# A hybrid decoder trunk on one core: attention scores of a head pair as one full-array product on a block diagonal key tile

## The chip, the cores and the metric

The kernel runs on one core of one Trainium2 chip. Such a core has a matrix engine (TensorE, PE in the profile, with its weight loads as PEld), a vector engine (VectorE, DVE), an activation engine (ScalarE, ACT), a general engine (GpSimd, POOL), and DMA queues that the sync engine (SyncE, SP) issues. The engines run side by side; each executes its own instructions in order and waits on semaphores of the others. The metric is the device time of one execution in microseconds (us), as a median over runs.

## What is computed

Two layers of a conditioned decoder trunk on 256 positions with width 1024. Each layer has a mixer, in which a gated delta rule branch (8 heads) and a sliding-window attention branch (16 query heads, 2 key heads, head width 64, window 128) stand side by side, and then a gated MLP of width 2816. All inputs and weights are fp32. The part of the reference that the change touches, cut:

```python
def swa_sink_attention(q, k, v, sinks):
    qb = q.astype(f32).reshape(B, nb, SWA_BLOCK, SWA_KV_HEADS, SWA_GROUP, D)
    kb, vb = band(k), band(v)
    s = jnp.einsum('bnqhgd,bnkhd->bnhgqk', qb, kb) * (D ** -0.5)
    ...
    s = jnp.where(mask[None, :, None, None], s, -jnp.inf)
    m = jnp.maximum(jnp.max(s, axis=-1, keepdims=True), sink)
    p = jnp.exp(s - m)
    denom = jnp.sum(p, axis=-1, keepdims=True) + jnp.exp(sink - m)
    o = jnp.einsum('bnhgqk,bnkhd->bnqhgd', p / denom, vb)
```

## The kernel before, in words

Most of the time goes to projections. A chunk of 128 x 1024 weights comes in by DMA as `raw`, ScalarE casts it to a reduced-precision high part `wH` (line 210), VectorE subtracts to get the low part `wL` (line 212), and `mm3` (lines 282 to 284) adds three products of 128 x 256 for each of the eight slices: high times high, high times low, low times high. The modulation vectors come from dot products of a 128 x 1024 chunk `wada` on VectorE (line 328), which shares the `raw` buffers.

Everything else of the mixer is put between these products. A small planner in the kernel (`Job`, `spawn`, `tick`, lines 230 to 258) advances generators by estimated cost and wait, a number pair at each `yield`; the framework's scheduler then sets each engine's final order, ahead of time, from the dependencies, buffers and priorities. Among the generators are the delta rule's two halves of four heads (`Half`: Gram products `ps_kk` at line 728, a blocked triangular inverse with the tiles `u`, `ut`, `yt` and products `ps_y`, `ps_z`, then the solve), and the attention.

The attention has two parts. `attention_prep(tb)` (line 932) normalizes and rotates queries and keys for one block of 128 positions and transposes them: `qT` holds for each of eight head pairs 128 rows, 64 of the even and 64 of the odd head; `kT` holds each key head's transposed keys twice, in rows 0 to 63 and again in rows 64 to 127. ScalarE copies the transposed keys from PSUM to `kT` (line 967).

`attention(tb, kv)` (line 969) is one unit: a block of 128 queries and a key head, that is eight query heads. There are four units per layer. The scores go to two tiles of four heads, `ps_cur0` for the even and `ps_cur1` for the odd heads, each 128 x 512. Line 975 issues eight products, one per head, alternating between the two tiles: 64 rows of `qT` as the stationary side, 64 rows of `kT` as the moving side with 128 columns. In the profile these have the tile `64*128`. A unit of the first block (tb = 0) has only this set; one of the second block has a second set against the previous block's keys (`ps_prv`, line 987), written over the masked places by `copy_predicated`. The tiles come from the PSUM pool `atps`, which has two buffers, shared with the value products `ps_o`, the transposed probabilities `ps_pT`, and tiles of the delta rule (`ps_vt`, `ps_n2`).

Then come maximum, exponential with the row sum, division (lines 994 to 1012), a transposition of the probabilities on PE (line 1016) into `pc` and, in the second block, `pp`, and the product with the values: line 1031, for even heads into partitions 0 to 63 of `ps_o` and for odd heads into 64 to 127, each of 512 columns (four heads at once), and line 1034 for the previous block, added on. In the profile these have the tile `128*64`.

Buffers that the change renames: `ssq` (line 411), a running sum of squares for the norms, has a tag of its own; `k2` (line 697), squares of keys in the delta rule, has one buffer; `pc` at line 442, a column of a rank-one correction, has four buffers of four bytes a partition.

Of the kernel before, what the change touches and what calls it, by code (L numbers as in the profile page):

```python
# [4 lines left out]
F32 = mybir.dt.float32  # L5
# [7 lines left out]
P = 128  # L13
T = 256
# [85 lines left out]
def trunk(tc, xT, cvec, pos, wada, wsa, wbig, wdn, par, cst, out):  # L100
# [15 lines left out]
    big = pool("big", 1)  # L116
    wk = pool("wk", 2)
# [291 lines left out]
    def ssq_add(kt):  # L409
        if kt == 0:  # L410
            s = wk.tile([P, T], F32, name="ssq", tag="ssq", bufs=1)
            A.activation(s, x[:, 0], AF.Square)
            ssq["t"] = s
        else:
            q = t1("sqx")
            A.activation(q, x[:, kt], AF.Square)
            V.tensor_tensor(ssq["t"], ssq["t"], q, ALU.add)

    class Raw:
# [16 lines left out]
        def proj(self, r, scale=1.0, alt=False):  # L436

            p_ = proj(lambda kt: self.h[:, kt, 0:T + 2], lambda kt: self.l[:, kt, 0:T + 2], T + 2, alt)
            with tc.high_priority(offset=HPN):
                t = t1("pr")  # L440
                V.tensor_tensor(t, p_[:, 0:T], r, ALU.mult)
                c = sm.tile([P, 1], F32, name="pc", bufs=4)
                A.activation(c, p_[:, T:T + 1], AF.Identity, scale=scale)
            return t, c
# [79 lines left out]
    for l in range(NL):  # L524
# [407 lines left out]
        def attention_prep(tb):  # L932
# [32 lines left out]
            for g in range(2):  # L965
                PE.transpose(pk[:, g], kd[:, g].rearrange("p a b -> p (a b)"), C("ident"))
            A.copy(kT[:, :, ts], pk)

        def attention(tb, kv):
            ts = slice(tb * P, tb * P + P)  # L970
            hfs = (slice(0, 64), slice(64, 128))
            pcur = [pat([4, P], name=f"ps_cur{i}") for i in range(2)]
            for j in range(4):
                for i in range(2):
                    PE.matmul(pcur[i][:, j], qT[hfs[i], kv * 4 + j, ts], kT[hfs[i], kv, ts], start=True, stop=True)  # L975
            s_ = [at2(f"s{i}") for i in range(2)]
# [3 lines left out]
            else:  # L980
                for i in range(2):
                    AB.copy(s_[i], pcur[i])
                yield 0.95, 1.2
                pprv = [pat([4, P], name=f"ps_prv{i}") for i in range(2)]
                for j in range(4):
                    for i in range(2):
                        PE.matmul(pprv[i][:, j], qT[hfs[i], kv * 4 + j, ts], kT[hfs[i], kv, 0:P],
                                  start=True, stop=True)
                for i in range(2):
# [4 lines left out]
            for i in range(2):  # L994
                s = s_[i]
                hs = slice(kv * 8 + i, kv * 8 + 8, 2)
                mx = sm.tile([P, 4], F32, name="mx", bufs=4)
# [8 lines left out]
                for j in range(4):  # L1006
                    after(AB.activation(s[:, j], s[:, j], AF.Exp, bias=nm[:, j:j + 1],
                                       scale=rq[:, tb, kv * 8 + i + 2 * j:kv * 8 + i + 2 * j + 1],
                                       accum_out=sme[:, j:j + 1]), last_silu[-1])
# [18 lines left out]
            po = pat([4, P], name="ps_o")  # L1028
            o = [po[i * 64:i * 64 + 64] for i in range(2)]
            for i in range(2):  # L1030
                PE.matmul(o[i], vtok[:, tb, vs], pcs[i], start=True, stop=tb == 0)  # L1031
            if tb:
                for i in range(2):
                    tc.keep_in_program_order(PE.matmul(o[i], vtok[:, 0, vs], pps[i], start=False, stop=True))
            ks = slice(kv * 4, kv * 4 + 4)
# [18 lines left out]
        qT = big.tile([P, 8, T], F32, name="qT", tag="s5")  # L1054
        kT = big.tile([P, 2, T], F32, name="kT", tag="kT")
        rq = sm.tile([P, 2, 16], F32, name="rq")
# [259 lines left out]
```

## Time and profile before

| | us |
|---|---|
| median of 3 runs | 1029.28 |
| lowest and highest run | 1028.52, 1032.02 |
| span of the profiled execution | 1029.4 |
| PE busy, of that span | 999.7 (97%) |
| VectorE busy | 843.6 (82%) |
| ScalarE busy | 631.2 (61%) |
| GpSimd busy | 4.0 |

No separate device time is given for the profiled execution beside its span. In a row of the timeline stand the start, the time, the engine, the line, the operation, output and inputs, the shape, a count, and in brackets the idle time ahead with what ended it. In a row of the groups the count is followed by the busy time in us, the mean of one in ns, and the idle time ahead. In a row of the windows stand the stretch, its length, then for each engine (PE, PEld, DVE, ACT, POOL, unless one is chosen) the busy time with the number of instructions, then the granted clock of PE, the share of the DMA engines, and GB/s. Helpers that raise an operation's priority stand under line 278.

### The profile page before, as it was taken

The page shows a single profiled execution, that of the slowest core. Times are in us where ns is not written, and L with a number is a line of the kernel's source. Part 1 is how long each engine was busy: PE and PEld are TensorE (multiplying, and loading weights), DVE is VectorE, ACT ScalarE, POOL GpSimd, SP SyncE. Part 2 cuts the span into 40 slices and gives each one's busy share as a digit, 9 for nine tenths or more (in the row PEclk, how much of TensorE's full clock was granted, in tenths as well). Part 3 has the DMA queues.
Part 4 walks back from the last instruction along what each step waited for, and adds up shares of the span by engine and source line. Part 5 has one row for each costly group of instructions (what it writes and reads, how often), then busy time and mean ns, then how long its engine had stood idle before and what let it go on. Part 6 is the DMA issues. An engine that isn't in the chain of part 4 may idle for free.

```text
span 1029.4 us, 23195 instructions
## 1 busy us (share of the span) xinstructions
PE 999.7 (97%) x9208; PEld 946.0 (92%) x9208; DVE 843.6 (82%) x1873; ACT 631.2 (61%) x1281; POOL 4.0 (0%) x8
## 2 busy tenths in 40 slices
PE   4999999999999999999999999999999999999998
PEld 2599998998899999999999999899879999999998
DVE  6799997799788898998996999986857889777653
ACT  5598675766555665564465977577554558555532
POOL 0000000000000000000000000000000000000000
PEclk9999998999999999999999999999999999999999
DMA  9875486537555478888976556762313655566661
GB/s 361 324 247 175 173 268 204 183 124 266 170 183 191 155 226 282 291 282 298 358 262 210 168 168 193 239 242 83 110 57 107 202 185 179 191 191 194 185 211 40
DMA packets 60444, 210.47 MB, mean 204 GB/s; under 512 B 6960, under 2 KB 8496, under 8 KB 60336
## 3 DMA queue, kind: packets, MB, share of 16 engines
q1 hardware_dynamic: 59904, 208.89, 61.3%
q8 instruction: 72, 1.18, 0.5%
q14 instruction: 36, 0.29, 0.1%
q10 hardware_dynamic: 432, 0.10, 0.0%
HBM read 207.92 MB, written 1.05 MB: 203 GB/s over the span
## 4 chain that ended last, share of the span: by engine, by line
PE 77%; DVE 13%; ACT 5%; DMA 2%; issue 2%; SPq 0%; DVEq 0%; ACTq 0%
PE acc L282 20%; PE acc L283 19%; PE acc L284 19%; DVE wL L212 4%; PE pa L567 4%; DMA raw<-wada 2%; ACT wH L210 2%; DVE raw L328 2%; PE ps_o L1031 1%; PE ps_kk L728 1%; DVE kq L672 1%; PE ps_cur L975 1%; PE pa L585 1%; PE pa L583 1%; PE pa L584 1%
## 5 line engine op out<-in xcount | busy, mean ns | idle before, releaser
L210 ACT CAST wH<-raw 128x1024 fp32r<-128x1024 f32 (+2 forms) x292 | 301.0, 1035 | 207.8 <-PE acc L283 130.0
L212 DVE TENSOR_TENSOR wL<-raw,wH 128x1024 fp32r<-128x1024 f32 (+2 forms) x292 | 349.3, 1200 | 76.2 <-ACT wH L210 73.3
L282 PE MATMUL acc<-hH,wH 128*128 128x256 f32 x1376 | 394.3, 287 | 0.0
L283 PE MATMUL acc<-hL,wH 128*128 128x256 f32 x1376 | 385.8, 280 | 0.0
L284 PE MATMUL acc<-hH,wL 128*128 128x256 f32 x1376 | 385.1, 280 | 0.3 <-DVE wL L212 0.2
L282 PEld LDWEIGHTS acc<-hH,wH 128*128 128x128 f32 x1376 | 259.9, 189 | 7.4 <-issue 4.3
L284 PEld LDWEIGHTS acc<-hH,wL 128*128 128x128 f32 x1376 | 260.1, 189 | 1.1 <-DVE wL L212 0.7
L283 PEld LDWEIGHTS acc<-hL,wH 128*128 128x128 f32 x1376 | 260.1, 189 | 0.7 <-issue 0.2
L328 DVE SCALAR_TENSOR_TENSOR raw<-raw,cact 128x1024 f32<-128x1024 f32 x80 | 97.1, 1219 | 9.2 <-DMA raw<-wada 9.1
L284 PE MATMUL acc<-g_b,wL 128*128 128x256 f32 x224 | 61.8, 276 | 0.0
L282 PE MATMUL acc<-g_b,wH 128*128 128x256 f32 x224 | 61.8, 276 | 0.0
L283 PE MATMUL acc<-g_b,wH 128*128 128x256 f32 x224 | 61.8, 276 | 0.0
L672 DVE SCALAR_TENSOR_TENSOR kq<-cr,pt,kq 128x255 f32<-128x255 f32 (+2 forms) x96 | 45.4, 479 | 1.5 <-ACT kq L670 1.5
L282 PEld LDWEIGHTS acc<-g_b,wH 128*128 128x128 f32 x224 | 42.1, 188 | 0.0
L283 PEld LDWEIGHTS acc<-g_b,wH 128*128 128x128 f32 x224 | 42.1, 188 | 0.0
L284 PEld LDWEIGHTS acc<-g_b,wL 128*128 128x128 f32 x224 | 42.1, 188 | 0.0
L567 PE MATMUL pa<-raw,h 128*128 128x432 f32 x96 | 37.5, 555 | 2.6 <-ACT h L473 2.6
L1192 DVE SCALAR_TENSOR_TENSOR g<-acc,pt,g 128x255 f32<-128x255 f32 x80 | 38.2, 478 | 0.6
L567 PEld LDWEIGHTS pa<-raw,h 128*128 128x128 f32 x96 | 19.2, 202 | 20.6 <-issue 17.2
L282 PE MATMUL acc<-sH,wH 128*128 128x256 f32 x128 | 36.7, 289 | 0.0
L284 PE MATMUL acc<-sH,wL 128*128 128x256 f32 x128 | 36.6, 287 | 0.0
L283 PE MATMUL acc<-sL,wH 128*128 128x256 f32 x128 | 36.5, 285 | 0.0
(329 smaller groups left out, 1964.0 us busy)
## 6 DMA issues: line engine op xcount, KB each, us to landing
raw<-wbig SPq DMA_DIRECT2D x232, 512.0 KB, 4.0
raw<-wada SPq DMA_DIRECT2D x80, 512.0 KB, 4.5
raw<-wdn SPq DMA_DIRECT2D x32, 512.0 KB, 4.5
raw<-wsa SPq DMA_DIRECT2D x24, 432.0 KB, 4.8
early<-wada SPq DMA_DIRECT2D x16, 512.0 KB, 8.5
raw<-wdn SPq DMA_DIRECT2D x16, 384.0 KB, 4.1
x<-xT SPq DMA_DIRECT2D x4, 256.0 KB, 4.2
out<-x SPq DMA_DIRECT2D x8, 128.0 KB, 3.0
```

The lines of the kernel that those rows point to most:

```text
L210: A.copy(h, raw)
L212: V.tensor_tensor(lo, raw, h.bitcast(F32), ALU.subtract)
L282: PE.matmul(o, wh, ah, start=first, stop=False)
L283: PE.matmul(o, wh, al, start=False, stop=False)
L284: PE.matmul(o, wl, ah, start=False, stop=last)
L328: return V.scalar_tensor_tensor(raw, raw, 1.0, cact, op0=ALU.mult, op1=ALU.mult, accum_out=modp[l][:, f:f + 1])
L567: PE.matmul(pa[g][tb], h32[:, tb * P:tb * P + P], w, start=n == 0, stop=n == KT - 1)
L583: PE.matmul(o, hh[:, kt, sl], wh[:, k4], start=kt == 0, stop=False)
L584: PE.matmul(o, hh[:, kt, sl], wl[:, k4], start=False, stop=False)
L585: PE.matmul(o, hl[:, kt, sl], wh[:, k4], start=False, stop=kt == KT - 1)
L672: V.scalar_tensor_tensor(dst[:, sft:], cr[:, :T - sft], w_[:, 3 - sft:4 - sft], dst[:, sft:], op0=ALU.mult, op1=ALU.add)
L1192: V.scalar_tensor_tensor(g[:, sft:], pa_[:, :T - sft], fw[:, i, 2 - sft:3 - sft], g[:, sft:], op0=ALU.mult, op1=ALU.add)
```

## The change

`kT` is replaced by `kbd`, a tile with, for each key head and each block of 128 keys, 256 columns: rows 0 to 63 hold the transposed keys in the first 128 columns, rows 64 to 127 hold them in the last 128, and the rest is zero, set once per layer by a memset on GpSimd. The copy from PSUM becomes two copies of 64 rows each. A product now takes all 128 rows of a head pair of `qT` as the stationary side and 256 columns of `kbd` as the moving side, and gives the scores of both heads of the pair next to each other: four products in place of eight for a set. So the heads lie in natural order in the score tiles, heads 0 to 3 of the unit in the first and 4 to 7 in the second, each tile filled by two products in a row. The slices of the sinks and of the scales follow. The value products take the even or odd heads of a tile by a stride of two, each with 256 columns, so twice as many. Besides, `ssq` shares the buffer of `k2`, and `pc` has three buffers.

```diff
     def ssq_add(kt):
         if kt == 0:
-            s = wk.tile([P, T], F32, name="ssq", tag="ssq", bufs=1)
+            s = wk.tile([P, T], F32, name="ssq", tag="k2", bufs=1)
...
-                c = sm.tile([P, 1], F32, name="pc", bufs=4)
+                c = sm.tile([P, 1], F32, name="pc", bufs=3)
...
-            A.copy(kT[:, :, ts], pk)
+            for i in range(2):
+                q = slice(i * 64, i * 64 + 64)
+                A.copy(kbd[q, :, tb, i], pk[q])
 
         def attention(tb, kv):
             ts = slice(tb * P, tb * P + P)
-            hfs = (slice(0, 64), slice(64, 128))
-            pcur = [pat([4, P], name=f"ps_cur{i}") for i in range(2)]
-            for j in range(4):
-                for i in range(2):
-                    PE.matmul(pcur[i][:, j], qT[hfs[i], kv * 4 + j, ts], kT[hfs[i], kv, ts], start=True, stop=True)
+
+            def scores(name, blk):
+                out = []
+                for b in range(2):
+                    o = pat([4, P], name=name)
+                    for p_ in range(2):
+                        PE.matmul(o[:, 2 * p_:2 * p_ + 2], qT[:, kv * 4 + 2 * b + p_, ts], kbd[:, kv, blk],
+                                  start=True, stop=True)
+                    out.append(o)
+                return out
+
+            pcur = scores("ps_cur", tb)
...
-                pprv = [pat([4, P], name=f"ps_prv{i}") for i in range(2)]
-                for j in range(4):
-                    for i in range(2):
-                        PE.matmul(pprv[i][:, j], qT[hfs[i], kv * 4 + j, ts], kT[hfs[i], kv, 0:P],
-                                  start=True, stop=True)
+                pprv = scores("ps_prv", 0)
...
-                hs = slice(kv * 8 + i, kv * 8 + 8, 2)
+                h0 = kv * 8 + 4 * i
+                hs = slice(h0, h0 + 4)
...
-                                       scale=rq[:, tb, kv * 8 + i + 2 * j:kv * 8 + i + 2 * j + 1],
+                                       scale=rq[:, tb, h0 + j:h0 + j + 1],
...
             po = pat([4, P], name="ps_o")
-            o = [po[i * 64:i * 64 + 64] for i in range(2)]
-            for i in range(2):
-                PE.matmul(o[i], vtok[:, tb, vs], pcs[i], start=True, stop=tb == 0)
-            if tb:
+            for b in range(2):
+                o = [po[i * 64:i * 64 + 64, 2 * b:2 * b + 2] for i in range(2)]
                 for i in range(2):
-                    tc.keep_in_program_order(PE.matmul(o[i], vtok[:, 0, vs], pps[i], start=False, stop=True))
+                    PE.matmul(o[i], vtok[:, tb, vs], pcs[b][:, i::2], start=True, stop=tb == 0)
+                if tb:
+                    for i in range(2):
+                        tc.keep_in_program_order(PE.matmul(o[i], vtok[:, 0, vs], pps[b][:, i::2], start=False, stop=True))
...
-        kT = big.tile([P, 2, T], F32, name="kT", tag="kT")
+        kbd = big.tile([P, 2, 2, 2, P], F32, name="kbd", tag="kbd")
+        G.memset(kbd, 0.0)
```

The new score products are line 979 of the changed kernel, the value products lines 1038 and 1041, the key copies line 969.

## The prediction

> **What bounds the kernel now.** I read the page first: the busy shares, the granted clock and the chain that ended last.
>
> ```profile
> PE 999.7 (97%) x9208; PEld 946.0 (92%) x9208; DVE 843.6 (82%) x1873; ACT 631.2 (61%) x1281; POOL 4.0 (0%) x8
> PEclk9999998999999999999999999999999999999999
> PE 77%; DVE 13%; ACT 5%; DMA 2%; issue 2%; SPq 0%; DVEq 0%; ACTq 0%
> ```
>
> The span is 1029.4 us, and TensorE (PE) is busy in 97% of it and carries 77% of the chain. So what counts is the time that PE's stream takes, and the few places where the stream stands still. Next come the groups of instructions on PE that the change touches; the last two numbers before the idle time are busy us and mean ns. An fp32 product leaves two records (128 records for the 64 products of L975).
>
> ```profile
> L975 PE MATMUL ps_cur<-kT,qT 64*128 64x128 f32 x128 | 16.0, 291 | 1.6 <-issue 1.6
> L1031 PE MATMUL ps_o<-pc,vtok 128*64 128x512 f32 x32 | 12.4, 618 | 0.0
> L987 PE MATMUL ps_prv<-kT,qT 64*128 64x128 f32 x64 | 7.1, 285 | 0.2 <-ACT s L278 0.2
> L1034 PE MATMUL ps_o<-pp,vtok 128*64 128x512 f32 x16 | 6.5, 598 | 0.0
> ```
>
> About 23 us of scores and 19 us of value products: 4% of the span. A mean of 291 ns is no price, since matmuls overlap; prices I take from starts in the timeline. Here are a half set (four products, one head parity), a whole set (eight, the parities alternating), and full-array fp32 products of 256 columns in another stage (two products).
>
> ```profile
> 220.21 0.28 PE L283 MATMUL acc<-hL,wH 128*128 128x256 f32 x1
> 220.33 0.28 PE L284 MATMUL acc<-hH,wL 128*128 128x256 f32 x1
> 220.54 1.16 PE L975 MATMUL ps_cur<-kT,qT 64*128 64x128 f32 x8
> 221.62 0.39 PE L282 MATMUL acc<-hH,wH 128*128 128x256 f32 x1
> 221.85 0.28 PE L283 MATMUL acc<-hL,wH 128*128 128x256 f32 x1
> ```
>
> ```profile
> 224.83 0.28 PE L284 MATMUL acc<-hH,wL 128*128 128x256 f32 x1
> 225.04 1.16 PE L987 MATMUL ps_prv<-kT,qT 64*128 64x128 f32 x16
> 226.13 0.39 PE L282 MATMUL acc<-hH,wH 128*128 128x256 f32 x1
> 226.36 0.28 PE L283 MATMUL acc<-hL,wH 128*128 128x256 f32 x1
> ```
>
> ```profile
> 106.87 0.28 PE L284 MATMUL acc<-hH,wL 128*128 128x256 f32 x1
> 106.98 1.03 PE L728 MATMUL ps_kk<-kq 128*128 128x256 f32 x4
> 107.66 0.47 PE L282 MATMUL acc<-hH,wH 128*128 128x256 f32 x1
> 107.97 0.28 PE L283 MATMUL acc<-hL,wH 128*128 128x256 f32 x1
> ```
>
> A projection product steps by 0.12 us (220.21 to 220.33). I price a block from the last product before it to the second behind it, less two such steps, which takes in what entering and leaving cost. The half set costs 221.85 - 220.33 - 0.24 = 1.28 us. The whole set, with twice the products, costs 226.36 - 224.83 - 0.24 = 1.29: products on the two 64-row halves run side by side only if they alternate. Two full-array products cost 107.97 - 106.87 - 0.24 = 0.86, that is 0.43 each.
>
> **Scores, product by product.** A unit of the first query block has one set, the current block's; a unit of the second has two, with the previous block's. Two units of each per layer make 6 sets, 12 in all. Whether a set is whole or split is decided by the order. On PE in layer 0, second unit, stood (ps_cur_2500 and ps_cur_2501 are the two score tiles):
>
> ```order
> L975 MATMUL ps_cur_2500<-kT,qT 128x128 x4
> L282 MATMUL acc<-hH,wH 128x256
> L283 MATMUL acc<-hL,wH 128x256
> L284 MATMUL acc<-hH,wL 128x256
> L282 MATMUL acc<-hH,wH 128x256
> L283 MATMUL acc<-hL,wH 128x256
> L284 MATMUL acc<-hH,wL 128x256
> L877 MATMUL ps_y_2520<-vt,um 128x128 x2
> L975 MATMUL ps_cur_2501<-kT,qT 128x128 x4
> ```
>
> and now, at the same place:
>
> ```order
> L979 MATMUL ps_cur<-kbd,qT 128x256 x2
> L282 MATMUL acc<-hH,wH 128x256
> L283 MATMUL acc<-hL,wH 128x256
> L284 MATMUL acc<-hH,wL 128x256
> L282 MATMUL acc<-hH,wH 128x256
> L283 MATMUL acc<-hL,wH 128x256
> L284 MATMUL acc<-hH,wL 128x256
> L877 MATMUL ps_y_2517<-vt,um 128x128 x2
> L979 MATMUL ps_cur<-kbd,qT 128x256 x2
> ```
>
> Four products of one parity wait together for the second buffer and so run alone; two full-array products take the place of each four. In the whole order 5 sets alternate and 7 are split. Three half sets late in layer 1 follow each other and share their entry:
>
> ```profile
> 753.92 0.82 PE L975 MATMUL ps_cur<-kT,qT 64*128 64x128 f32 x5
> ...
> 756.89 0.69 PE L828 MATMUL ps_z<-u,yt 32*32 32x32 f32 x32
> ```
>
> They take 2.97 us and not 3 x 1.28 = 3.84. Before: 5 x 1.29 + 14 x 1.28 - 0.87 = 23.5 us. After: 48 x 0.43 = 20.6. **-2.9 us.** A whole set gets dearer (1.72 for 1.29) and a split one cheaper (1.72 for 2.56).
>
> The Trainium skill, "TensorEngine Tiling (Array Packing)", When to Use Tiling, says that a contraction of 64 should use two row tiles, which may give up to twice the speed. By it the old form would be the better one, by 12 x (1.72 - 1.29) = 5.2 us; the trace agrees for the 5 alternating sets and not for the 7 split ones.
>
> **Value products.** They go from 24 of 512 columns to 48 of 256, as many columns. A pair on the two column halves and a single product cost alike:
>
> ```profile
> 192.07 0.28 PE L284 MATMUL acc<-hH,wL 128*128 128x256 f32 x1
> 192.28 1.08 PE L1031 MATMUL ps_o<-pc,vtok 128*64 128x512 f32 x4
> 193.29 0.38 PE L282 MATMUL acc<-hH,wH 128*128 128x256 f32 x1
> ```
>
> ```profile
> 242.57 1.07 PE L1031 MATMUL ps_o<-pc,vtok 128*64 128x512 f32 x2
> 243.57 0.75 PE L787 MATMUL ps_y<-ut,lq 32*32 32x32 f32 x64
> ```
>
> 1.01 us for the pair, 1.00 for one alone: each broken pair costs another 1.0. On PE in layer 0, third unit (ps_y: the inverse's products), stood
>
> ```order
> L1031 MATMUL ps_o<-pc,vtok 64x512
> L787 MATMUL ps_y_3251<-ut_3243,lq 32x32 x32
> L1031 MATMUL ps_o<-pc,vtok 64x512
> L1034 MATMUL ps_o<-pp,vtok 64x512 x2
> L282 MATMUL acc<-hH,wH 128x256
> ```
>
> and now
>
> ```order
> L1038 MATMUL ps_o<-pc,vtok 64x256 x2
> L1041 MATMUL ps_o<-pp,vtok 64x256
> L787 MATMUL ps_y_3242<-ut_3234,lq 32x32 x32
> L1041 MATMUL ps_o<-pp,vtok 64x256
> L1038 MATMUL ps_o<-pc,vtok 64x256 x2
> L1041 MATMUL ps_o<-pp,vtok 64x256 x2
> ```
>
> The broken pair is now of half the columns. Layer 1 has two such places, so 3 x 0.5 = 1.5 us go. Against this stand 24 more products, whose start no row shows at 256 columns on half the array; bounds are 0 and 24 x 0.07 = 1.7 (an estimate: the pair's 1.01 is two passes after one another, 0.50 each, where 512 columns take 0.43 on the full array). Most of that 0.07 is the entry into the half array, paid once a block, so I take 0.3, near nothing. **-1.2 us.**
>
> **What lies beside PE.** The key copy is cut in two:
>
> ```profile
> L967 ACT COPY kT<-ps_kT x4: 372/372/373, 100.7 to 615.0; 128x256 f32<-128x256 f32 x4
> ```
>
> Four more copies of at most 0.37 are 1.5 us of ScalarE (ACT), busy 61%; behind them wait the weight casts (wH). Bounds 0 and +1.5; I take **+0.3**. The two memsets of kbd go to GpSimd (POOL), whose eight instructions took 4.0 us in all; one stands first in its queue and the other between memsets of the inverse, both long ahead of a reader: nothing, at most their own 1 us each if a score waited. The shared buffers (ssq with k2, three pc) meet in stages that don't overlap: nothing.
>
> **The order in layer 0.** At the first score set stand two stalls:
>
> ```profile
> 164.38 0.71 PE L975 MATMUL ps_cur<-kT,qT 64*128 64x128 f32 x6
> 166.71 1.13 PE L975 MATMUL ps_cur<-kT,qT 64*128 64x128 f32 x10 [1.62 <-issue]
> ...
> 168.37 0.41 PE L284 MATMUL acc<-hH,wL 128*128 128x256 f32 x1
> 169.19 0.34 PE L820 MATMUL ps_y<-ut,lq 32*32 32x32 f32 x5 [0.41 <-DVE ut L278]
> ```
>
> ```profile
> 167.46 1.23 DVE L328 SCALAR_TENSOR_TENSOR raw<-raw,cact 128x1024 f32<-128x1024 f32 x1 [2.81 <-DMA raw<-wada]
> ```
>
> The second: ps_y waits for ut, and ut stands on VectorE (DVE) behind a modulation dot that waits 2.81 us for its DMA. The difference on DVE there (u and ut: the inverse; - before, + now):
>
> ```order
>  L352 SCALAR_TENSOR_TENSOR a_0_109<-mod_102,pt 128x4
> -L278 SCALAR_TENSOR_TENSOR u_1527<-ps_z_2089,ct,u_1527 128x8x16
> -L328 SCALAR_TENSOR_TENSOR raw,modp_104<-raw,cact 128x1024
> -L278 STREAM_TRANSPOSE ut_2148<-u_1527 128x256
> +L278 SCALAR_TENSOR_TENSOR u_1530<-ps_z_2092,ct,u_1530 128x8x16
> +L212 TENSOR_TENSOR wL<-raw,wH 128x1024
>  L672 SCALAR_TENSOR_TENSOR vv<-cr,pt,vv 128x255
> ```
>
> The dot (L328) no longer stands between u and ut; it comes later, when the data has long landed. The wait of 169.19 - 168.37 - 0.12 = 0.7 us goes: **-0.7** (bounds 0, if the wL now ahead is late, and -0.7). The first stall is "issue", inside a run of products that waits for no engine. Six passes stand ahead of it; in the whole set above 16 took 225.04 to 226.13, 0.07 each, and in the new form one takes 0.215. If the stall ends at a fixed moment, 166.71, the new passes fill 6 x (0.215 - 0.07) = 0.9 us of it, less 0.1 for the entry that they don't pay: **-0.8** (bounds 0, if it moves along, and -1.6, if it goes).
>
> **The sum.** -2.9 - 1.2 + 0.3 - 0.7 - 0.8 = -5.3. Some comes back as waits where PE now arrives earlier at ACT or DVE; I take 0.7, from this row of the stage of layer 1 with its scores, where 1.75 us of PE idle time exist already:
>
> ```profile
> 675.00:775.00 100.00, 98.25 (x1111) 1.00 0.32 108
> ```
>
> -4.6 us. The profiled span of 1029.4 is 0.1 above the median of the runs, 1029.28, so I set it against the median: **1024.7 us**. About 0.3% (3.1 us) is what a measurement of this kernel can tell from no change; the runs themselves lay between 1028.52 and 1032.02.
>
> **Rivals.** *Only the stream gets shorter, and part is handed back*: the two order terms don't come, ACT's copies cost their 1.5 and waits return 0.9: -2.9 - 1.2 + 1.5 + 0.9 = -1.7, 1027.6 us. For it: the order of DVE and ACT in layer 0 is shuffled widely from 100 us on, and DVE is in the chain there. Against: the products themselves are priced by rows. Chance 0.30.
>
> *The clock stays up*: behind the stalls at 164 to 169 us the clock falls:
>
> ```profile
> 163.70:167.10 3.40, 1.78 (x18) 1.45 (x20) 0.88 (x5) 3.05 (x7) 0.00 (x0) 1.00 0.87 312
> 167.10:173.90 6.80, 6.39 (x86) 5.61 (x84) 5.54 (x14) 1.27 (x4) 0.00 (x0) 0.50 0.38 133
> ```
>
> After a stretch with PE busy 1.78 of 3.40, 6.8 us run at clock 0.50. With the stalls shortened that stretch would be busy for some 2.6, and at full clock the 6.39 would take 3.2 less; I count 3.0. 1024.7 - 3.0 = 1021.7 us. Against: how much idle time brings the clock down isn't seen. Chance 0.17. The Trainium skill, "TensorE: Matmul & The Clock Gate", Part 1, says that free-running windows of about 3.4 us decide, one idle window bringing half clock; the length agrees with the row, and by it the phase, not the kernel alone, settles this rival.
>
> *Half A comes late* (the other side): the last of its Gram products (ps_kk) moved 23 products back on PE, 23 x 0.12 = 2.7 us, and its inverse starts from that. If its products stand where they stood, PE waits the 2.7, and a second stretch at half clock costs another 3.2: -1.7 + 2.7 + 3.2 = +4.2, 1033.5 us. It decides from about 2 us of wait on. Against: the first ps_y moved back by 12 products too. Chance 0.05.
>
> *The row tiles were the better form*: if the split halves ran side by side after all, -2.9 becomes +5.2, and with -1.2 for the values the time is 1033.3. Against: the 1.28 of a half set. Chance 0.03.
>
> The forecast keeps 0.45. Faster by over 0.3%: forecast and clock, 0.62; within: 0.30; slower: 0.05 + 0.03 = 0.08. The range, 1020.8 to 1029.2, takes in the clock's case with 0.9 of spread and the first rival up to where nothing is gained.
>
> **What would show it.** Right: full-array score blocks of 0.86 us for two, no step of 0.2 into and out of them; broken value pairs of 0.5; no DVE wait for wada ahead of ut near 167 us. Wrong: a full-array pair over 1.0, PE idle time over 30 us in all, new waits of PE on ut, on s or on casts in the layer 0 mixer, or half clock in more windows than two.

## The result and the profile after

| | before | after |
|---|---|---|
| median, us (runs) | 1030.96 (22) | 1024.95 (22) |
| lowest and highest run, us | 1026.96, 1034.67 | 1022.92, 1031.25 |
| ratio of after to before | | 0.995, 95% interval 0.9935 to 0.9964 |
| time and span of the profiled execution, us | span 1029.4 | 1022.96, span 1021.1 |

The changed kernel is faster, by 3.7 to 6.7 us at the ends of the interval. A second measurement of the same kernel gave 0.9944 (0.9915 to 0.9972). The forecast was 1024.7, or 4.6 less than before; measured are 5.2 by the ratio and 6.0 by the medians. That the time itself came out within 0.3 us is luck: the prediction started from a median of three runs, 1029.28, and with more runs the kernel before lies at 1031.0. The base was 1.7 us too low and the gain 1.4 us too small, and the two errors cancel. It also set its span against that median, where the profiled execution of after took 1.9 us more than its span. So the terms are looked at one by one.

The page of after first: busy times, the clock in 40 slices, and the chain that ended last.

```profile
PE 992.3 (97%) x9160; PEld 944.0 (92%) x9160; DVE 842.8 (83%) x1873; ACT 633.1 (62%) x1285; POOL 5.9 (1%) x10
PEclk9999999999999999999999999999999999999999
PE 67%; DVE 17%; ACT 6%; DMA 6%; issue 4%; SPq 0%; DVEq 0%; ACTq 0%
```

TensorE still bounds the kernel, with the same 97%. Its share of the chain differs from profile to profile (67% here, 70% in a second profile of the changed kernel, 77% before); whether the score products lie on the path is tested directly by e3. The clock row has no 8 any more: this execution had no stretch at half clock, where the one of before had 6.8 us at 167 and 3.4 us at 652. (The second profile of the changed kernel has two of 3.4 us, at 486 and 654.)

The same timeline as in the prediction, of after: two full-array products where a half set stood, a set of four products, and the first set of layer 0.

```profile
214.04 0.28 PE L284 MATMUL acc<-hH,wL 128*128 128x256 f32 x1
214.16 1.03 PE L979 MATMUL ps_cur<-kbd,qT 128*128 128x256 f32 x4
214.84 0.47 PE L282 MATMUL acc<-hH,wH 128*128 128x256 f32 x1
215.14 0.28 PE L283 MATMUL acc<-hL,wH 128*128 128x256 f32 x1
...
241.28 0.29 PE L284 MATMUL acc<-hH,wL 128*128 128x256 f32 x1
241.41 1.89 PE L979 MATMUL ps_cur<-kbd,qT 128*128 128x256 f32 x8
242.95 0.47 PE L282 MATMUL acc<-hH,wH 128*128 128x256 f32 x1
243.25 0.28 PE L283 MATMUL acc<-hL,wH 128*128 128x256 f32 x1
```

By the prediction's own rule (from the last product ahead to the second behind, less 0.24) the pair costs 215.14 - 214.04 - 0.24 = 0.86 us and the set 243.25 - 241.28 - 0.24 = 1.73, as priced. The step into the block is 0.12, not 0.2.

```profile
162.72 1.46 PE L979 MATMUL ps_cur<-kbd,qT 128*128 128x256 f32 x6
165.07 0.70 PE L979 MATMUL ps_cur<-kbd,qT 128*128 128x256 f32 x2 [0.89 <-issue]
...
165.84 0.28 PE L284 MATMUL acc<-hH,wL 128*128 128x256 f32 x1
166.05 0.69 PE L820 MATMUL ps_y<-ut,lq 32*32 32x32 f32 x32
```

The "issue" stall inside the first set is still there, 0.89 us in place of 1.62 (1.27 in the second profile). The wait of ps_y for ut is gone: L820 has no bracket. On VectorE:

```profile
162.04 1.23 DVE L328 SCALAR_TENSOR_TENSOR raw<-raw,cact 128x1024 f32<-128x1024 f32 x1 [0.86 <-DMA raw<-wada]
...
163.59 0.35 DVE L278 SCALAR_TENSOR_TENSOR u<-ps_z,ct,u 128x128 f32<-128x128 f32 x1
163.85 1.22 DVE L212 TENSOR_TENSOR wL<-raw,wH 128x1024 fp32r<-128x1024 f32 x1
164.98 0.48 DVE L672 SCALAR_TENSOR_TENSOR vv<-cr,pt,vv 128x255 f32<-128x255 f32 x1
165.37 0.44 DVE L278 STREAM_TRANSPOSE ut<-u 128x256 f32<-128x256 f32 x1
```

No dot stands between u and ut any more. One still stands ahead of u and waits 0.86 us for its DMA, but ut comes in time for ps_y. The value products at the place of the order that the prediction quoted:

```profile
236.37 0.28 PE L284 MATMUL acc<-hH,wL 128*128 128x256 f32 x1
236.57 0.65 PE L1038 MATMUL ps_o<-pc,vtok 128*64 128x256 f32 x4
237.06 0.59 PE L1041 MATMUL ps_o<-pp,vtok 128*64 128x256 f32 x2
237.58 0.75 PE L787 MATMUL ps_y<-ut,lq 32*32 32x32 f32 x64
```

The pair of halves takes 237.06 - 236.57 = 0.49 us, the broken one behind it 0.52. Priced block by block, all value products cost 15.1 us against 16.6 before, and all score products 23.7 against 26.8.

### The profile page after: what moved, and what is told of

Its sections match the earlier page's. It is cut to its first block, busy times and chain, and to the rows that moved or that the text cites. A ratio compares the mean times of both kernels' runs of the same rounds, so it can differ in the third digit from the quotient of the medians.

```text
span 1021.1 us, 23111 instructions
## 1 busy us (share of the span) xinstructions
PE 992.3 (97%) x9160; PEld 944.0 (92%) x9160; DVE 842.8 (83%) x1873; ACT 633.1 (62%) x1285; POOL 5.9 (1%) x10
## 4 chain that ended last, share of the span: by engine, by line
PE 67%; DVE 17%; ACT 6%; DMA 6%; issue 4%; SPq 0%; DVEq 0%; ACTq 0%
PE acc L282 17%; PE acc L283 17%; PE acc L284 17%; DVE wL L212 6%; PE pa L567 4%; DMA raw<-wada 3%; ACT wH L210 2%; DVE raw L328 2%; DVE kq L672 1%; DMA raw<-wdn 1%; PE ps_kk L728 1%; PE pa L585 1%; PE pa L584 1%; PE pa L583 1%; DVE vv L672 1%
## 5 line engine op out<-in xcount | busy, mean ns | idle before, releaser
L284 PE MATMUL acc<-g_a,wL 128*128 128x256 f32 x128 | 35.6, 278 | 0.8 <-DVE wL L212 0.8
```

The source lines that it names most:

```text
L284: PE.matmul(o, wl, ah, start=False, stop=last)
```

## The experiments

Each run of the study lists the clock that TensorE was granted on average, and the runs of most kernels spread over 7 to 12 us. The table sets both side by side, for the 240 runs whose clock is listed. A fit through all of them, with one slope and a level for each kernel, gives 0.85 us (0.76 to 0.94) for 0.001 of mean clock. (An estimate to set beside it: 0.001 of a span of 1030 us is 1.03 us of TensorE's time at most.) The last column is the level of each kernel against the one before, that is the difference at equal clock, with its 95% interval. The 96 runs of the kernel before are from four chips, with medians of 1030.6, 1030.7, 1030.9 and 1031.7; at equal clock the four differ by 0.6 us at most.

| kernel | runs | median, us | ratio to before (interval) | mean clock | at equal clock, us |
|---|---|---|---|---|---|
| before | 96 | 1030.9 | | 0.9970 | 0 |
| changed (both measurements) | 29 | 1025.0 | 0.995, 0.9944 | 0.9985 | -4.0 ± 0.7 |
| e1: second score tile from the other pool | 12 | 1031.7 | 0.9997 (0.9974 to 1.002) | 0.9922 | -4.3 ± 1.1 |
| e2: key tile alone | 12 | 1030.7 | 0.999 (0.9969 to 1.0012) | 0.9964 | -1.2 ± 1.0 |
| e3: score products doubled | 4 | 1049.6 | 1.0172 (1.0141 to 1.0203) | 0.9970 | +18.2 ± 1.6 |
| e4: dot held | 12 | 1029.2 | 0.9983 (0.9965 to 1.0001) | 0.9976 | -1.3 ± 1.0 |
| e5: changed, dots behind vv | 12 | 1026.6 | 0.995 (0.9929 to 0.9971) | 0.9972 | -3.9 ± 1.0 |
| e7: e1 and e4 | 12 | 1029.6 | 0.9989 (0.9968 to 1.001) | 0.9923 | -4.5 ± 1.1 |
| e8: values in halves | 12 | 1033.0 | 1.0015 (0.9994 to 1.0036) | 0.9967 | +1.3 ± 1.0 |
| e10: e7 without the last two units | 12 | 1028.7 | 0.9975 (0.9956 to 0.9995) | 0.9958 | -3.9 ± 1.0 |
| e11: e1 in the last two units alone | 12 | 1032.4 | 1.0011 (0.9991 to 1.0032) | 0.9945 | -1.4 ± 1.0 |
| e12: both forms | 9 | 1026.1 | 0.9956 (0.9939 to 0.9972) | 0.9944 | -6.9 ± 1.1 |
| e13: both forms, first set full | 6 | 1022.6 | 0.9914 (0.9889 to 0.994) | 0.9987 | -7.4 ± 1.3 |

### e1: whole row-tiled sets, without the change

```diff
-            pcur = [pat([4, P], name=f"ps_cur{i}") for i in range(2)]
+            pcur = [(pat, ps)[i]([4, P], name=f"ps_cur{i}") for i in range(2)]
...
-                pprv = [pat([4, P], name=f"ps_prv{i}") for i in range(2)]
+                pprv = [(pat, ps)[i]([4, P], name=f"ps_prv{i}") for i in range(2)]
```

In the kernel before, a set is split because its second tile waits for the buffer of the first. Here the second comes from the other PSUM pool, and 9 of 12 sets alternate.

> The kernel before, with one edit: the second score tile of a set comes from the delta rule's PSUM pool, so that both tiles are there at once and the row-tiled products alternate. In its order 9 of 12 sets alternate and 3 are split. Theory of the prediction (PE's stream counts, a half set costs as much as a whole one): 4 more alternating sets at 1.29 for 2.56 us, 4 to 5 us less than before, as much as the change brings. Rival (the gain came from the order in layer 0 and the clock, the product's form is worth little): within 1 us of before.

No gain was measured: 0.9997 (0.9974 to 1.002). Yet the sets got as short as a whole row-tiled set was priced (timeline of e1):

```profile
190.85 0.28 PE L284 MATMUL acc<-hH,wL 128*128 128x256 f32 x1
191.06 1.16 PE L975 MATMUL ps_cur<-kT,qT 64*128 64x128 f32 x16
192.16 0.39 PE L282 MATMUL acc<-hH,wH 128*128 128x256 f32 x1
192.38 0.28 PE L283 MATMUL acc<-hL,wH 128*128 128x256 f32 x1
```

192.38 - 190.85 - 0.24 = 1.29, and all score blocks together 21.8 us, 5.0 less than before and 1.8 less than after. What ate it stands in the windows and the timeline near the end of layer 1's mixer:

```profile
742.97:746.38 3.41, 3.41 (x83) 2.42 (x78) 3.09 (x6) 2.43 (x5) 0.00 (x0) 1.00 0.58 204
746.38:749.79 3.41, 3.41 (x110) 2.40 (x98) 1.80 (x5) 1.31 (x3) 0.00 (x0) 1.00 0.77 259
749.79:753.20 3.41, 2.40 (x65) 1.94 (x65) 1.55 (x5) 3.06 (x8) 0.00 (x0) 1.00 0.09 32
753.20:766.85 13.65, 13.65 (x104) 12.51 (x98) 2.77 (x11) 6.14 (x21) 0.00 (x0) 0.50 0.00 1
```

```profile
747.56 0.71 PE L975 MATMUL ps_cur<-kT,qT 64*128 64x128 f32 x4
748.20 0.75 PE L794 MATMUL ps_z<-u,yt 32*32 32x32 f32 x64
748.88 1.16 PE L975 MATMUL ps_cur<-kT,qT 64*128 64x128 f32 x12
749.97 0.69 PE L820 MATMUL ps_y<-ut,lq 32*32 32x32 f32 x32
750.60 1.16 PE L987 MATMUL ps_prv<-kT,qT 64*128 64x128 f32 x16
752.62 1.00 PE L828 MATMUL ps_z<-u,yt 32*32 32x32 f32 x22 [0.86 <-ACT yt L278]
```

From 744.9 to 751.8 us, the end of it shown, only products on parts of the array stand there, without one projection product, then a wait; and then 13.7 us run at clock 0.50. In the table e1 is level with the changed kernel at equal clock (-4.3 against -4.0) and has the lowest clock of all, 0.9922. So the price of the split sets fits, and the gain from mending them was lost to the clock. Neither theory of the expectation had that.

### e2: the key tile alone

```diff
...
-                    PE.matmul(pcur[i][:, j], qT[hfs[i], kv * 4 + j, ts], kT[hfs[i], kv, ts], start=True, stop=True)
+                    PE.matmul(pcur[i][:, j], qT[hfs[i], kv * 4 + j, ts], kbd[hfs[i], kv, tb, i], start=True, stop=True)
...
```

The memsets, the copies in two and the shared buffers of the change, with the old products reading their half of kbd.

> The kernel before with the key tile of the change (memset, two copies, shared buffers), but the old row-tiled products, which read their 64 rows of it. VectorE and ScalarE then have the order of the changed kernel up to the first units. Theory of the prediction: only the order term and the copies, -0.7 + 0.3, so 0 to 1 us less than before; the changed kernel stays 4 us faster. Rival (order and clock made the gain): 3 to 5 us less than before, near the changed kernel.

-1.2 ± 1.0 us at equal clock; 0.999 (0.9969 to 1.0012). VectorE's order near the first set is that of the changed kernel, so this contains what the dot's place is worth (e4: -1.3); copies and memsets themselves come out at 0.1 ± 1.4. The other 2.8 of the 4.0 us that the change gains at equal clock come with the products.

### e3: the score products twice

```diff
                     for p_ in range(2):
-                        PE.matmul(o[:, 2 * p_:2 * p_ + 2], qT[:, kv * 4 + 2 * b + p_, ts], kbd[:, kv, blk],
-                                  start=True, stop=True)
+                        for _ in range(2):
+                            PE.matmul(o[:, 2 * p_:2 * p_ + 2], qT[:, kv * 4 + 2 * b + p_, ts], kbd[:, kv, blk],
+                                      start=True, stop=True)
```

The changed kernel with each of its 48 score products issued twice.

> The changed kernel with every score product issued twice. Theory of the prediction: 48 more products at 0.43 us on a stream that bounds, 20 to 21 us more than the changed kernel, 15 to 16 more than before. Rival (the attention's products lie in waits that exist anyway): 10 us more than the changed kernel or less.

At equal clock it lies 18.2 + 4.0 = 22.2 ± 1.7 us above the changed kernel, 0.46 for each added product where 0.43 was the price. The score products are paid in full on the path.

### e4: the dot's place alone

```diff
-                if behind:
-                    after(dot, behind["op"])
+                if behind or (l, g, f) == (0, 4, 4):
+                    after(dot, behind["op"] if behind else late["ut64"])
...
-                VB.transpose(ut.rearrange("p a b -> p (a b)"), u32.rearrange("p a b -> p (a b)"))
+                late["ut64"] = VB.transpose(ut.rearrange("p a b -> p (a b)"), u32.rearrange("p a b -> p (a b)"))
```

One modulation dot is held behind ut on VectorE; the products on PE keep their order.

> The kernel before with one modulation dot held behind the transpose ut of the inverse on VectorE in layer 0; PE and ScalarE keep their order. Theory of the prediction: the wait of 0.7 us on PE at 168 us goes, 0.7 us less than before. Rival (idle time on PE brings the clock down, so its cost is the half clock behind it): one stretch of 3.4 us less at half clock, 2 to 3 us less than before.

0.9983 (0.9965 to 1.0001), -1.3 ± 1.0 us at equal clock, and the wait of ps_y is gone in its trace. By the medians that is within the noise; the forecast's -0.7 lies inside both.

### e5: the other dot that stands ahead of a tap

```diff
-                    after(dot, behind["op"])
+                    after(dot, late["vv5"] if (l, g) == (1, 3) and f > 4 else behind["op"])
...
-                    V.scalar_tensor_tensor(dst[:, sft:], cr[:, :T - sft], w_[:, 3 - sft:4 - sft], dst[:, sft:],
+                    late[f"vv{hd}"] = V.scalar_tensor_tensor(dst[:, sft:], cr[:, :T - sft], w_[:, 3 - sft:4 - sft], dst[:, sft:],
```

> The changed kernel with one more edit: the modulation dots of columns (1,3,5) to (1,3,7) may not stand ahead of the last tap of vv of head 5. In the changed kernel's trace such a dot (1.22 us) stands between two taps at 645.0 us, the vv transposes (L703) come 1.97 us after the last projection product, and nothing else was waited for there. Theory (waits on an in-order VectorE are paid in full by TensorE, which is 97% busy): the stall of 1.97 us falls to 0.7 or less, the time is 1.2 us less than that of the changed kernel of the same chip and call, about 1.5 with what a half-clock stretch behind it costs in some runs; ratio against the kernel before about 0.9935. Rival (given back: the dot is only late somewhere else): within 0.5 us of the changed kernel, with another stall of over 1 us within the next 40 us.

The wait fell, and another came (timeline of e5):

```profile
647.87 0.44 PE L703 MATMUL ps_vt<-ct,vv 128*128 128x128 f32 x2 [0.87 <-ACT vv L674]
...
677.90 0.41 PE L703 MATMUL ps_vt<-ct,vv 128*128 128x128 f32 x2 [1.19 <-DVE s L278]
```

0.87 for the 1.69 of the changed kernel, and 1.19 at 678 for 0.24. It isn't faster than the changed kernel measured beside it, 1026.57 against 1025.74, and level with it at equal clock (-3.9, -4.0). So the rival has it: what was saved at one place came back at another. Behind the new wait its profile has 13.7 us at half clock, from 679.1 on. Which instruction on VectorE made s late there was not tried.

### e7: whole row-tiled sets and the dot held

The edits of e1 and e4 together.

> The kernel before with both edits of earlier runs: the second score tile from the other pool (whole row-tiled sets, no gain in the median when alone: 1031.73 us at a mean clock of 0.992) and the dot (0,4,4) held behind the ut transpose (1029.17 us when alone). Theory C (the gain of the whole sets is there, but TensorE stalls of over 1 us at 165 to 169 and 751 bring half-clock stretches that eat it): with the first stalls shorter the mean clock is 0.995 or more and the time 1026 to 1028 us; at a clock of 1.0 about 1023.3 (1025.1 of the first edit less 1.8). Rival (row-tiled sets themselves hold the clock down, stalls or not): mean clock stays near 0.992 and the time near 1030. If the sets' gain was never there: 1029.2, the time of the dot alone, at the same clock as that.

The mean clock stayed at 0.9923, the time at 1029.55, and a stretch of 13.7 us stands at 749.6 behind the same row of small products. Holding the dot didn't bring the clock back, and at equal clock it adds nothing to e1 (-4.5, -4.3). So the wait for ut near 168 is not what lowers the clock of e1.

### e8: the value products in halves, scores as before

```diff
-            o = [po[i * 64:i * 64 + 64] for i in range(2)]
-            for i in range(2):
-                PE.matmul(o[i], vtok[:, tb, vs], pcs[i], start=True, stop=tb == 0)
+            for b in range(2):
+                o = [po[i * 64:i * 64 + 64, 2 * b:2 * b + 2] for i in range(2)]
+                for i in range(2):
+                    PE.matmul(o[i], vtok[:, tb, vs], pcs[i][:, 2 * b:2 * b + 2], start=True, stop=tb == 0)
...
```

> The kernel before with only the value products cut in two: per half of the columns the two row-split products stand next to each other (four products of 256 columns where two of 512 stood), scores as before. Theory (the prediction's term: pairs that are not kept together pay twice, halves keep them): value products 16.6 us in the trace of before become about 15.1, time 1.2 us less, ratio 0.9988, with a span of 1.0 us either way for the order that the scheduler makes anew. Rival (the pairs are broken by when the probabilities come, not by the width): 16.5 us or more in the trace, ratio 1.000 or more; four products pay one more entry and exit each.

1.0015 (0.9994 to 1.0036), +1.3 ± 1.0 us at equal clock, and 16.9 us of value products in its trace: no gain. Here is why, from its timeline:

```profile
238.28 0.28 PE L284 MATMUL acc<-hH,wL 128*128 128x256 f32 x1
238.49 0.65 PE L1032 MATMUL ps_o<-pc,vtok 128*64 128x256 f32 x2
239.06 0.39 PE L282 MATMUL acc<-hH,wH 128*128 128x256 f32 x1
239.28 0.28 PE L283 MATMUL acc<-hL,wH 128*128 128x256 f32 x1
```

One product (two records) stands alone and costs 239.28 - 238.28 - 0.24 = 0.76, since the two products of a half read two tiles of probabilities that come at different times; there are 16 blocks in place of 11. In the changed kernel both read the same tile.

### e9: the changed kernel again

> The changed kernel again, unaltered, as the partner of the first run of this call: 1025 us, ratio 0.995 against the kernel before. Theory C (half-clock stretches make the spread): runs at a mean clock of 1.0 lie at 1022.9 to 1025.0, and each 0.001 of clock costs about 1 us. Rival (the spread is not the clock): runs at 1.0 spread as widely as the rest.

0.9944 (0.9915 to 0.9972), 1025.74 us. Its runs at a mean clock of 1.0 took 1023.9 and 1024.3 us, and with the eight of the first measurement they lie between 1022.9 and 1025.0. All 29 runs of the changed kernel have a clock of 0.996 or more, where 26% of the runs of before have 0.995 or less.

### e10 and e11: one place of e7 undone, and one place of e1 alone

```diff
-            pcur = [(pat, ps)[i]([4, P], name=f"ps_cur{i}") for i in range(2)]
+            pcur = [(pat, pat if (l, kv) == (1, 1) else ps)[i]([4, P], name=f"ps_cur{i}") for i in range(2)]
```

and in e11 `ps if (l, kv) == (1, 1) else pat`; the tiles of the previous block likewise. Both are shown against the kernel before; e10 also has the edit of e4.

> The kernel of the run with both edits (second score tile from the other pool, dot held), but the last two units of layer 1 (kv 1, in the trace at 737 to 755 us) take both tiles from the one pool as before. In the earlier orders with the other pool everywhere, 11 blocks of 32x32, score and value products follow each other there without one projection product between them, and both profiles show a half-clock stretch of 13.7 us right behind (753.2 and 749.6); here a projection block stands inside again. By all 154 timed runs so far, 0.001 of mean clock goes with 0.88 us, and at equal clock the kernel with both edits is 4.7 us ahead of the one before. Theory C (that one place brings the clock down): mean clock 0.996 to 0.998, time 1026 to 1028 us (1028.4 less 3.9, and 2.6 for the clock), no 13.7 us stretch near 750. Rival (whole row-tiled sets hold the clock down wherever they stand): mean clock about 0.992, time 1030 to 1031.

> The kernel before with the second score tile from the other pool in the last two units of layer 1 alone: TensorE's order differs from that of before only near 745 to 755 us, where the 11 blocks now stand without a projection product between them. Theory C: mean clock falls to 0.992 or 0.993, a stretch of 13.7 us stands in the profile near 750, and the time is 1033 to 1035 us although the score products there get 0.8 us shorter. Rival (the place is not the cause): mean clock 0.997 as before, time 1029.9.

e10: mean clock 0.9958 with a standard error of 0.0008 (e7: 0.9923, 0.0008), 1028.7 us. e11: 0.9945, error 0.0009 (before: 0.9970, 0.0002), 1032.4 us. Both moved the way that the place near 750 us would have it, by about three errors of the difference each, but neither by all that was expected, and e11's profile shows no stretch there. e10's profile has one of 10.2 us behind the first set, at 168. That fits a place that is one of several to bring the clock down, in some executions and not in others.

### e12 and e13: both forms in one kernel

```diff
+            ts, nat = slice(tb * P, tb * P + P), (l, kv) == (1, 1)
...
+                out = [(pat, pat if nat else ps)[b]([4, P], name=name) for b in range(2)]
+                for a, b in ((a, b) for a in range(2 if nat else 4) for b in range(2)):
+                    q = slice(b * 64, b * 64 + 64)
+                    args = ((out[a][:, 2 * b:2 * b + 2], qT[:, kv * 4 + 2 * a + b, ts], kbd[:, kv, blk]) if nat else
+                            (out[b][:, a], qT[q, kv * 4 + a, ts], kbd[q, kv, blk, b]))
+                    PE.matmul(*args, start=True, stop=True)
...
```

Full-array pairs in the last two units of layer 1 (`nat`), whole row-tiled sets in the other six, with the heads and value products of either form. e13 adds the first unit of layer 0: `or (l, tb, kv) == (0, 0, 0)`.

> The changed kernel, but only the last two units of layer 1 use full-array pairs and natural head order; the other six use row-tiled products on the same key tile, in the old head order, with the second score tile from the other pool and value products of 512 columns. Whole row-tiled sets take 1.29 us in the traces, full-array sets 1.73, two half sets 2.57. Theory: the stream is 0.5 to 1 us shorter than that of the changed kernel, the clock is that of the kernel before or better (0.997 to 0.9985) since projection products stand between the blocks at 745 to 755: 1025 to 1026.5 us. If the clock falls to 0.992: 1030. If the clock is that of the changed kernel (0.9985): 1024.5, and it would be the fastest.

> The hybrid with the first unit of layer 0 as full-array pairs too (eight products where sixteen stood behind the stall of 1.82 us at 164 us, ahead of its half-clock stretch of 6.8 us at 167.7); five units keep row-tiled products. The stream gets 0.4 us longer for that set (1.73 for 1.29). Theory (the thinly filled place at 161 to 168 us brought the stretch): the mean clock rises from 0.9944 to 0.997 or more, and the time is 1023.5 to 1024.5 us, the fastest of all (1028.4 less 6.5, and 1.5 to 2.5 for the clock). Rival (the stretch comes with the stall alone, whatever the products are, or the low clock of the hybrid has other places): clock about 0.994 to 0.995, time 1026 to 1026.5, no faster than the changed kernel.

e12 has the shorter stream (-6.9 at equal clock) and a clock of 0.9944: 1026.1 us, no better than the changed kernel. e13 keeps the stream (-7.4) and has 0.998 or more in all six runs: 1022.6 us, 0.9914 (0.9889 to 0.994), the fastest kernel of the study. The windows of e12 around the first set, then those of e13 (each as the stretches at half clock divide the execution, see the last section):

```profile
164.28:167.69 3.41, 1.86 (x73) 1.50 (x59) 3.34 (x9) 3.10 (x7) 0.00 (x0) 1.00 0.84 235
167.69:174.52 6.83, 6.83 (x77) 6.10 (x79) 3.31 (x8) 1.14 (x3) 0.00 (x0) 0.50 0.40 160
```

```profile
161.77:165.18 3.41, 3.05 (x78) 2.37 (x76) 3.34 (x9) 3.09 (x8) 0.00 (x0) 1.00 0.90 280
165.18:168.59 3.41, 2.92 (x48) 2.70 (x49) 3.41 (x8) 1.44 (x4) 0.00 (x0) 1.00 0.86 336
```

With the row-tiled set PE is busy for 1.86 of 3.41 us and the next 6.8 run at half clock; with the full-array set it is busy for 3.05 and 2.92 and they don't. In these two profiles the form of the products is not the only difference: the stall is 0.85 us in place of 1.55, and an edge between two windows falls into it. Over all runs the edit of that one unit raised the clock, from 0.9944 to 0.9987; the kernel before had 0.9968 beside the one and 0.9965 beside the other, and PE's order differs otherwise only in a few places between 179 and 246 us.

## Why the prediction was right, step by step

**Scores, -2.9.** The prices of a pair (0.86) and a set (1.73) held to 0.01. In sum the blocks went from 26.8 to 23.7 us; without what the longest step of the first set takes beyond a normal one (1.8 before, 1.1 after) from 25.0 to 22.6, -2.4. But the first set of before ran in part at half clock: e4, with the same order on PE and that set at full clock, has 24.5. So the products are worth -1.9, a third less than priced. Both sums are above the 23.5 and 20.6 of the working, by 1.0 and 2.0, since blocks between small products cost more than in the projection (the pair at 744.5 us of after 1.25); the working left that out, and the new form pays more of it. That score products are paid on the path e3 shows, at 0.46 each.

**Value products, -1.2.** -1.4 in the blocks of the trace. The reason was half right: that the broken pair has half the columns gains nothing by itself (e8, +1.3 ± 1.0). It is the natural order of heads that keeps the two products of a half together.

**Key copies and memsets, +0.3.** 0.1 ± 1.4 (e2 less e4): nothing that can be seen.

**The order on VectorE, -0.7.** The wait is gone, and the dot's place alone is worth -1.3 ± 1.0 (e4), which has the 0.7 inside but is no fine measure of it. Of the 0.7 in the row itself 0.41 is idle time, the bracket; the row lies in a stretch at half clock, where a projection product steps by 0.21 us and not by the 0.12 that was taken off.

**The first stall, -0.8.** Its bracket fell from 1.62 to 0.89. Beyond a normal step the longest one takes 1.8 us before and 1.1 after, and from the start of the set to the end of the stall it is 2.33 and 2.35 us: in this pair the reason holds, and the size. But the stall doesn't end at a fixed moment in general. In the second profile of the changed kernel it takes 2.73 us to its end and 1.4 beyond a normal step, and in e4, in the old form, 1.67 and 1.2. So the -0.8 is what these two profiles have; over all profiles the term isn't fixed.

**Handed back, +0.7.** Not to be told apart: span less busy time of PE is 28.8 us after and 29.7 before. Two of the signs that the prediction named as its refutation did come, small: in the layer 0 mixer PE waits anew for ut, 0.4 us in two waits at L787 and 0.3 at L843 (and 0.5 for yt, 0.2 for sL), where 0.4 for ut at L820 and 0.2 for wL went; and in the second profile the idle time is 32.2 us, over the 30 named, with a wait of 2.0 for wL in the MLP of layer 0 that the first doesn't have. So some was handed back, as the sum had it, and the forecast stands all the same.

At equal clock the sum is -4.0 ± 0.7 where -4.6 stood. An estimate from the terms, with -1.9, -1.4, 0.1, the prediction's own -0.7 and +0.7 for the order and for what is handed back, and -0.4 to -0.8 for the stall, comes to -3.6 to -4.0. **The clock** was the mistake of form: I put it as a rival that excludes the forecast (another -3.0, chance 0.17). It came, but as a shift of how often stretches at half clock occur: the mean clock rose from 0.9970 to 0.9985, worth 1.5 x 0.85 = 1.3 us. Together -5.3; the medians differ by 5.9.

**"The row tiles were the better form"** was turned down for the 1.28 of a half set, and for the kernel as it stood that is right. But with a second PSUM buffer the old form is the cheaper one, 1.29 for 1.73 a set. At equal clock e12 and e13, which use it for most units, lie 2.9 ± 1.3 and 3.4 ± 1.4 us under the changed kernel; e1, with 3 sets still split and the value products of before, is level with it. That the row tiles are the cheaper form agrees with what the Trainium skill, "TensorEngine Tiling (Array Packing)", When to Use Tiling, advises for a contraction of 64. What e1 won by it was lost to the clock.

## What to carry to other kernels

Price a block of products from starts, neighbours included, and ask what splits it: here a buffer that came free late cost as much as the products, and either a form that doesn't need the pair or another buffer mended it. When a kernel is bound by TensorE, list the granted clock with each run and compare kernels at equal clock as well as by medians: e1 was 4.3 us better in its stream and no faster. A wait that stands among products on parts of the array is a place to try full products: in e13 that one set went with a clock of 0.9987 for 0.9944. Both forms can stand in one kernel, each where it does best.

## What the runs showed of the hardware

The stretches at half clock last 3.4, 6.8, 10.2 or 13.7 us, multiples of 3.41, on a single core in the middle of a busy kernel. They also begin on a grid: in each of the 14 profiles every one begins a whole number of 3.413 us after the moment from which the clock is full for the first time (in before 20.31 us, and the stretch at 167.08 comes 43 such windows later). That moment lies between 18.4 and 21.5 us, so the grid falls otherwise against the work in each profile. The Trainium skill, "TensorE: Matmul & The Clock Gate", Part 1, gives the window as about 3.4 us and free-running, which agrees, and says that an idle window of that length throttles. No window ahead of a stretch was idle here, but for the waits in the last 21 us of the kernel.

Counted on the grid, busy time tells nearly all. Of the windows at full clock in the 14 profiles, but for the last 21 us of each, 16 have PE busy for 1.9 us or less, and 14 of them are followed by a stretch. Of all the others 3 are, with 2.22 (e5) and twice 2.41 us (e1, e7), and these three stretches last 13.7 us each. The two of the 16 that nothing follows have 1.58 us (e10, at 113) and 1.86 (e2, at 115). The changed kernel shows both sides at one place, its wait of L703 for vv. In the first profile the wait is 1.69 us long, and the next window has the full clock:

```profile
643.61:647.02 3.41, 1.91 (x17) 1.71 (x15) 3.41 (x9) 1.21 (x4) 0.00 (x0) 1.00 0.74 243
```

In the second it is 2.31 us long, and the next window has half of it:

```profile
650.13:653.54 3.41, 1.34 (x12) 1.34 (x13) 3.41 (x7) 1.08 (x3) 0.00 (x0) 1.00 0.66 241
653.54:656.96 3.42, 3.42 (x19) 3.42 (x18) 3.18 (x7) 1.34 (x3) 0.00 (x0) 0.50 0.65 217
```

How long PE waits, and whether an edge of the grid cuts the wait in two, would explain that stretches come in some executions of a kernel and not in others. Why the five exceptions are exceptions, and whether the rows and columns in use count beside the busy time, no run here separates. That stays open.

The stall inside the first set, which the profile puts down to "issue", appears in every kernel of the study, whatever form the products have, with a longest step between 0.8 and 1.9 us. In all 14 profiles it stands behind the third product of the set, in either form: at one place in PE's sequence of instructions, not at one moment. What it is was not tried.
